# Banks shared between Winograd products, later operand conversions and an earlier last sum in the down-projection of a one-core trunk kernel

## The chip, the cores and the metric

One core of a Trainium2 chip runs the whole program. The metric is the device time of one execution in microseconds (us). The engines are named as in the profile: PE (matrix multiplies, with PEld for its weight loads), DVE (vector), ACT (scalar), POOL (GpSimd) and SP (DMA issue).

## The reference, cut to what matters

One layer over 1024 tokens with 1024 channels: attention and a gated merge, then a gated MLP with a short convolution, then a final RMSNorm. The change lies in the last two steps:

```python
D_MODEL, SEQ, D_FF, EPS = 1024, 1024, 2816, 1e-6
# u: gate and value after the up-projection and the causal convolution
x = x + (jax.nn.silu(gate) * val) @ w_down[l]     # (1024, 2816) @ (2816, 1024)
...
def rmsnorm(x, w):
    y = x * lax.rsqrt(jnp.mean(x * x, axis=-1, keepdims=True) + EPS)
    return y * w
return rmsnorm(x, norm_final_w)
```

## The kernel before, in words

Everything is kept transposed: channels on the 128 partitions, tokens along the free dimension, and the 1024 tokens are two halves of 512. The float32 operands are each split into a high and a low part: ACT casts the high part (lines 127, 157, 175 for weights, 831 for hidden activations) and DVE subtracts it to get the low part (lines 128, 158, 177 and 832). Such a cast and subtraction together are called a **conversion** below. One product of four 128-row blocks then takes 12 matmuls of 128x512: high by high, high by low and low by high for each block (`product`, lines 918 to 920; with `low_last` the low weights come last, lines 912 and 914).

The down-projection (`down`) sums over 22 blocks of 128 hidden rows. Six blocks are done plainly (line 1157), then two **groups** of eight blocks are done by Winograd's form of Strassen's scheme. In it an output **pair** m (0 to 3) holds the channel blocks m and m+4, and the four quarters of its result are `col(m, 0)`, `col(m, 1)`, `col(m + 4, 0)` and `col(m + 4, 1)` of the accumulator `x3` (tile `x`, 128x512 each). Seven products replace eight: P1 = A11·B11, P2 = A12·B21, P3 = S4·B22, P4 = A22·T4, P5 = S1·T1, P6 = S2·T2, P7 = S3·T3. The A and S are weights and weight differences (POOL makes the S, lines 103 to 109 and 148 to 151), the B and T are hidden activations and their differences.

Every product lands in a PSUM bank. There are four banks of tag `d` and four of tag `y`. An **addition** is one DVE instruction that adds a bank into a quarter of `x3`. In the first group the loop before has done P1 and P2 with two additions a pair; the loop over pairs in the diff does P5, P6, P3, P4, P7. P1, P6 and P7 of a pair pile up in its `y` bank and are read out on the way; P5, P3 and P4 each have a `d` bank of their own. That loop has seven additions a pair: two at line 1235, one each at 1237, 1240 and 1243, and two at 1248.

Between these, `diffs(k)` forms the differences of the second group's activations (lines 1203 to 1206), and `prepare` queues the second group's conversions. Their 28 buffers are the ones that the first group's operands hold, so each conversion waits until PE has read a given operand for the last time: B11 takes T1's place, B21 T2's, T4 B22's, T2 T4's, T3 T3's own; T1 and B22 of the second group take the raw buffers. The weight buffers `wh` (A11/A12 and A22) and `sh` (S) have two copies each, the raw weight buffers three, the POOL sums `c` two. So a weight's conversion waits for PE, a DMA for conversions, and POOL for DMA and DVE.

The order of each engine's instructions is set by the framework's scheduler from the order in the code, with priorities and `issue_after` edges; each engine then runs its queue strictly in that order. At the end, `last_norm` sums squares over channels with matmuls against a column of ones (line 218), makes the reciprocal root on DVE and POOL (lines 225 and 227), spreads it by transposes (line 233) and multiplies the result (line 1361). The first half of the tokens is normalized beside the second group's last products, the second half in two quarters of 256 tokens. ACT takes the squares (line 1261) and the weighting by the norm's vector (line 1265).

Of the kernel before, what the change touches and what calls it, by code (L numbers as in the profile page):

```python
# [10 lines left out]
F32 = mybir.dt.float32  # L11
# [33 lines left out]
class Trunk:  # L45
# [92 lines left out]
    def second_pair(self, src, m):  # L138

        nc = self.nc  # L140
        raws = []
        for x in src:
            raws.append(self.tl(self.wp, [P, 8, P], "raw", bufs=RAW))
            nc.sync.dma_start(raws[-1], x)
        g, v = (r.rearrange("p (k a) c -> p a k c", a=2) for r in raws)
        sa, sb = (self.tl(self.sfp[0], [P, 2, 4, P], self.sfp[1]) for _ in range(2))
        tt = nc.gpsimd.tensor_tensor
        tt(sa[:, 0], v[:, 0], v[:, 1], ALU.add)
        tt(sb[:, 0], sa[:, 0], g[:, 0], ALU.subtract)
        tt(sb[:, 1], g[:, 0], v[:, 0], ALU.subtract)  # L150
        tt(sa[:, 1], g[:, 1], sb[:, 0], ALU.subtract)
        nc.sync.dma_start(self.sd[m], sa.rearrange("p a k c -> p (a k) c"))
        ops = {}
        for pool, h, l, x, names in ((self.wp, "wh", "wl", g, ("A11", "A12")), (self.uw, "sh", "sl", sb, ("S2", "S3")), (self.wp, "wh", "wl", v[:, 1:2], ("A22",))):
            hi = self.tl(pool, [P, len(names), 4, P], h, F32R)
            lo = self.tl(pool, [P, len(names), 4, P], l, F32R)
            nc.scalar.copy(hi, x)
            nc.vector.tensor_tensor(lo, x, hi.bitcast(F32), ALU.subtract)
            for i, name in enumerate(names):
                ops[name] = hi[:, i], lo[:, i]  # L160
        return ops
# [59 lines left out]
    def rstd_cols(self, ssq_ps, n, width):  # L221

        nc = self.nc
        ms = self.tl(self.st, [P, 8], "ms")
        nc.vector.tensor_scalar(ms[:, :n], ssq_ps[:, :n], 1.0 / width, EPS, ALU.mult, ALU.add)  # L225
        rs = self.tl(self.st, [P, 8], "rs")
        self.pow = nc.gpsimd.tensor_tensor(rs[:, :n], ms[:, :n], self.mhalf[:, :n], ALU.pow)  # L227
        return rs
# [821 lines left out]
    def sums_h(self, k):  # L1050

        b11, b12, b22, b21 = (self.raw_h(N1 + j, hf) for j, hf in ((k, 0), (k, 1), (k + 4, 1), (k + 4, 0)))
        tt = self.nc.vector.tensor_tensor
        tt(b11, b12, b11, ALU.subtract)
        self.B["T1", k] = self.parts_h(b11)
        tt(b12, b22, b12, ALU.subtract)
        tt(b22, b22, b11, ALU.subtract)
        self.B["T2", k] = self.parts_h(b22)
        self.B["T3", k] = self.parts_h(b12)
        tt(b21, b22, b21, ALU.subtract)  # L1060
        self.B["T4", k] = self.parts_h(b21)

    def glu(self, j, w, us, tp, after):
# [44 lines left out]
    def down(self):  # L1108

        nc, tc = self.nc, self.tc  # L1110
        with ExitStack() as ctx:
# [80 lines left out]
            def load(k):  # L1192

                r = self.slot(base + 2 * k), self.slot(base + 2 * k + 1)
                for o in range(2):
                    nc.sync.dma_start(r[o].rearrange("p a b -> p (a b)"), self.hd[N2 + 2 * k + o])
                raws[k] = [x[:, i] for x in r for i in range(2)]

            def diffs(k, after):

                b11, b12, b21, b22 = raws[k]
                with tc.issue_after(after.ins):
                    tt(b11, b12, b11, ALU.subtract)
                    tt(b12, b22, b12, ALU.subtract)
                    tt(b22, b22, b11, ALU.subtract)
                    tt(b21, b22, b21, ALU.subtract)
# [20 lines left out]

            for k in range(4):
                load(k)
            for m, y in enumerate(ys):  # L1230
                w = self.next_w()
                ps = bank(0)
                self.product(ps, w["S1"], "T1")
                for x in (col(m, 1), col(m + 4, 1)):
                    tt(x, x, ps, ALU.add)
                self.product(y, w["S2"], "T2", first=False, skip=True)
                tt(col(m, 1), col(m, 1), y, ALU.add)
                ps = bank(0)
                self.product(ps, w["S4"], "B22")
                tt(col(m, 1), col(m, 1), ps, ALU.add)  # L1240
                ps = bank(0)
                self.product(ps, w["A22"], "T4")
                i = tt(col(m + 4, 0), col(m + 4, 0), ps, ALU.subtract)
                if m in (1, 2):
                    diffs(2 * m - 1, i)
                self.product(y, w["S3"], "T3", first=False, skip=True)
                for hf in range(2):
                    i = tt(col(m + 4, hf), col(m + 4, hf), y, ALU.add)
                if m < 2:
                    diffs(2 * m, i)  # L1250
            prepare(24)
            q = H2 // 2
            seen = []
# [1 line left out]
            def evac(ps, m, hf, a=0, b=H2, last=False):  # L1255

                x = x3[:, m, hf * H2 + a:hf * H2 + b]
                tt(x, x, ps, ALU.add)
                sum_ = box[hf][:, a:b]
                sq = box[2 + len(seen) % 2][:, a:b] if hf in seen else sum_  # L1260
                nc.scalar.activation(sq, x, AF.Square)
# [3 lines left out]
                nc.scalar.mul(x, x, self.vecs[:, C_NO + m:C_NO + m + 1])  # L1265
                return sq

            ys, ws = [], []

# [5 lines left out]
            for m in range(4):  # L1275
                w = self.next_w()
                ws.append(w)
                y, ps = bank(1), bank(0)
                ys.append(y)
                self.product(y, w["A11"], "2B11", skip=True, low_last=True)  # L1280
                tt(col(m, 0), col(m, 0), y, ALU.add)
# [12 lines left out]
            tail = self.last_norm(psD, [box[0]], x3, 0, 0, H2, ((0, 2, nc.vector), (6, 8, nc.gpsimd), (2, 4, nc.vector), (4, 6, nc.vector)))  # L1294
# [134 lines left out]
```

## Time and profile before

| | |
|---|---|
| time, median of 3 runs | 1343.62 us (1343.31 to 1343.88) |
| time of the profiled execution | 1343.35 us |
| its span in the profile | 1341.1 us, so 2.25 us lie around it |
| PE busy | 1321.7 us (99% of the span) |
| DVE, ACT, POOL busy | 1065.8, 621.7, 495.6 us |
| mean granted PE clock | 0.995 |

PE is nearly always busy; it is idle for longer than a matmul only at the start, in the passage from the first to the second group (1250 to 1259 us) and at the end (from 1330 us). In rows of the timeline the first two numbers are the start and the duration in us; a bracket holds the idle time before the row and what ended it.

### The profile page before, as it was taken

How to read it: one execution, taken by the hardware profiler on the slowest of the kernel's cores; microseconds unless marked ns; L12 is line 12 of the kernel's file. 1: busy time of each engine (PE TensorE's matmuls, PEld its weight loads, DVE VectorE, ACT ScalarE, POOL GpSimd, SP SyncE). 2: the span in 40 equal slices, each digit the busy share in tenths (PEclk: the TensorE clock that was granted, in tenths of full speed). 3: DMA queues.
4: the chain of work that ended last, by engine and by line, in shares of the span. 5: the costliest groups of instructions: out<-in, count | busy, mean ns of one | idle time of the engine just before them, and what ended most of it. 6: DMA issues, size and time to landing. Idle time of an engine off the chain costs nothing.

```text
span 1341.1 us, 17306 instructions
## 1 busy us (share of the span) xinstructions
PE 1321.7 (99%) x6264; PEld 1097.4 (82%) x6264; DVE 1065.8 (79%) x1603; ACT 621.7 (46%) x1019; POOL 495.6 (37%) x365
## 2 busy tenths in 40 slices
PE   7999999999999999999999999999999999999997
PEld 6888888888888778878888888888888888888787
DVE  8847775289889876465678999999999987869975
ACT  8432232276667665333454444334444434323443
POOL 0336552000102124641446555655556510224412
PEclk9999999999999999999999999999999999999998
DMA  6423443966553235334423222222222239562333
GB/s 258 148 104 150 149 157 141 254 174 188 143 138 130 93 121 200 138 110 157 141 96 108 65 93 90 83 81 77 95 79 90 75 116 330 202 246 71 113 115 126
DMA packets 63045, 182.64 MB, mean 136 GB/s; under 512 B 6896, under 2 KB 15216, under 8 KB 62960
## 3 DMA queue, kind: packets, MB, share of 16 engines
q1 hardware_dynamic: 51504, 164.13, 37.3%
q10 hardware_dynamic: 11456, 17.41, 3.6%
q8 instruction: 49, 0.80, 0.2%
q14 instruction: 36, 0.29, 0.1%
HBM read 130.66 MB, written 50.86 MB: 135 GB/s over the span
## 4 chain that ended last, share of the span: by engine, by line
PE 86%; DVE 5%; POOL 4%; DMA 2%; issue 2%; ACT 1%; POOLq 0%; SPq 0%; ACTq 0%; DVEq 0%
PE t L920 13%; PE t L919 13%; PE t L918 13%; PE g L210 3%; PE g L211 3%; PE g L212 3%; PE t L912 3%; PE sc L634 3%; PE y L1157 2%; PE d L1157 2%; PE sc L212 2%; PE sc L210 2%; PE sc L211 2%; DMA gr<-gd 2%; PE d L918 2%
## 5 line engine op out<-in xcount | busy, mean ns | idle before, releaser
L1087 ACT ACTIVATE c<-us,vecs 128x512 f32<-128x512 f32 x80 | 61.3, 781 | 132.3 <-POOL us L1081 128.3
L1089 DVE SCALAR_TENSOR_TENSOR c<-us,vecs,c 128x512 f32<-128x512 f32 x160 | 110.4, 747 | 8.6 <-ACT c L1087 8.5
L1081 POOL TENSOR_TENSOR us<-us,rstd 128x1024 f32<-128x1024 f32 x38 | 99.6, 2642 | 4.5 <-DVE us L467 2.4
L128 DVE TENSOR_TENSOR sl<-sf,sh 128x1024 fp32r<-128x1024 f32 x62 | 87.6, 1416 | 11.5 <-ACT sh L127 11.5
L127 ACT CAST sh<-sf 128x1024 fp32r<-128x1024 f32 x62 | 63.4, 1048 | 60.4 <-PE t L919 44.0
L177 DVE TENSOR_TENSOR wl<-raw,wh 128x1024 fp32r<-128x1024 f32 (+2 forms) x46 | 57.7, 1255 | 30.2 <-ACT wh L175 18.9
L128 DVE TENSOR_TENSOR wl<-raw,wh 128x1024 fp32r<-128x1024 f32 (+1 forms) x35 | 75.9, 2169 | 3.7 <-ACT wh L127 3.6
L103 POOL TENSOR_TENSOR sf<-rv 128x512 f32<-128x512 f32 x30 | 41.3, 1377 | 100.9 <-DVE sl L128 57.8
L175 ACT CAST wh<-raw 128x1024 fp32r<-128x1024 f32 (+2 forms) x46 | 46.0, 1001 | 62.6 <-PE sc L211 30.5
L210 PE MATMUL g<-xh,wh 128*128 128x512 f32 x176 | 70.7, 402 | 0.1
L212 PE MATMUL g<-xh,wl 128*128 128x512 f32 x176 | 70.4, 400 | 0.0
L211 PE MATMUL g<-xl,wh 128*128 128x512 f32 x176 | 70.3, 400 | 0.0
L108 POOL TENSOR_TENSOR sf<-raw,rv 128x512 f32<-128x512 f32 x30 | 40.7, 1356 | 65.4 <-DVE sl L128 65.4
L617 POOL MEMSET aT<- 128x128 f32 x32 | 6.1, 205 | 151.5 <-PE t L663 63.2
L638 DVE CUSTOM_DVE_ANT_0 L<-sc,bias 128x128 f32<-128x128 f32 (+7 forms) x64 | 47.7, 751 | 17.0 <-PE sc L634 13.7
L639 ACT ACTIVATE L<-L,sm 128x128 f32<-128x128 f32 (+7 forms) x64 | 49.6, 778 | 20.0 <-DVE sm L638 13.5
L792 POOL TENSOR_TENSOR gr<-gr,rstd 128x1024 f32<-128x1024 f32 x16 | 40.4, 2533 | 41.2 <-DMA gr<-gd 40.9
L1091 ACT ACTIVATE c<-c 128x512 f32<-128x512 f32 x40 | 24.0, 600 | 60.7 <-DVE c L1089 60.7
L128 DVE TENSOR_TENSOR wl<-rv,wh 128x512 fp32r<-128x512 f32 x30 | 49.2, 1640 | 3.5 <-ACT wh L127 3.5
L634 PE MATMUL sc<-u,u 128*128 128x512 f32 (+2 forms) x192 | 49.7, 358 | 0.0
L212 PE MATMUL sc<-mh,wl 128*128 128x512 f32 x126 | 49.1, 390 | 0.3 <-DVE wl L177 0.3
L227 POOL TENSOR_TENSOR rs<-ms,mhalf 128x8 f32<-128x8 f32 (+2 forms) x9 | 13.6, 1517 | 96.5 <-DVE ms L225 85.9
(522 smaller groups left out, 4429.6 us busy)
## 6 DMA issues: line engine op xcount, KB each, us to landing
u<-qd SPq DMA_DIRECT2D x72, 256.0 KB, 6.0
raw<-in_w_in SPq DMA_DIRECT2D x25, 512.0 KB, 4.1
raw<-in_w_up SPq DMA_DIRECT2D x23, 512.0 KB, 3.5
hr<-hd SPq DMA_DIRECT2D x46, 256.0 KB, 5.2
hd<-c SPq DMA_DIRECT2D x22, 512.0 KB, 2.6
rv<-in_w_up SPq DMA_DIRECT2D x21, 512.0 KB, 3.5
raw<-in_w_down SPq DMA_DIRECT2D x19, 512.0 KB, 4.1
gr<-gd SPq DMA_DIRECT2D x16, 512.0 KB, 3.5
```

The source lines that it names most:

```text
L127: i = nc.scalar.copy(hi, src)
L128: j = nc.vector.tensor_tensor(lo, src, hi.bitcast(F32), ALU.subtract)
L210: nc.tensor.matmul(ps, wh[:, kc + o, :], ah, start=first and n == 0, stop=False)
L211: nc.tensor.matmul(ps, wh[:, kc + o, :], al, start=False, stop=False)
L212: nc.tensor.matmul(ps, wl[:, kc + o, :], ah, start=False, stop=last and n == len(kcs) - 1)
L634: nc.tensor.matmul(sc[:, lo + n0:lo + n1], qs, k[c][part][:, n0:n1], start=part == 0, stop=part == 1)
L918: nc.tensor.matmul(ps, ah[:, k, :], bh, start=first and n == 0, stop=False, skip_group_check=skip)
L919: nc.tensor.matmul(ps, ah[:, k, :], bl, start=False, stop=False, skip_group_check=skip)
L920: i = nc.tensor.matmul(ps, al[:, k, :], bh, start=False, stop=last and n == len(ks) - 1, skip_group_check=skip)
L1081: (nc.vector if j == 0 else nc.gpsimd).tensor_tensor(u[:, 2:], u[:, 2:], self.rstd, ALU.mult)
L1087: nc.scalar.activation(c, u[:, o + 2:o + 2 + H2], AF.Identity, bias=self.vecs[:, C_CB + m:C_CB + m + 1], scale=col(m, 2))
L1089: nc.vector.scalar_tensor_tensor(c, u[:, o + k:o + k + H2], col(m, k), c, ALU.mult, ALU.add)
```

## The change: what it does

- **First group.** P5 is added to one quarter only, and P3 then accumulates onto P5's bank, whose sum is added to `col(m, 1)`. P4 accumulates onto P7's bank `y`, one pair later (`fourth(m - 1)`); its sum is the only addition to `col(m + 4, 0)`. T4 gets the opposite sign, so that it is added. With the two additions of the loop before this makes seven a pair; pair 3 has P4 in a bank of its own and one more. The loop goes from 28 additions to 21. PE's order of products becomes P5, P6, P4 of the pair before, P3, P7.
- **diffs** are placed at other points of that loop.
- **Second group.** `prepare(4)` queues T1's and B22's conversions behind those of the weights of the last pair asked for (`self.made`).
- **The end.** In the last two quarters, the weighting of the last two blocks is queued behind the last square. The ones-matmuls go over the squares first and over the two 128-token columns second, with one bank for each column, and the mean is taken by two small DVE instructions.

The core of the diff:

```diff
@@ second_pair
-            nc.scalar.copy(hi, x)
-            nc.vector.tensor_tensor(lo, x, hi.bitcast(F32), ALU.subtract)
+            self.made = nc.scalar.copy(hi, x), nc.vector.tensor_tensor(lo, x, hi.bitcast(F32), ALU.subtract)
@@ rstd_cols
-        nc.vector.tensor_scalar(ms[:, :n], ssq_ps[:, :n], 1.0 / width, EPS, ALU.mult, ALU.add)
+        parts = ssq_ps if isinstance(ssq_ps, list) else [ssq_ps[:, :n]]
+        w = n // len(parts)
+        for i, x in enumerate(parts):
+            nc.vector.tensor_scalar(ms[:, i * w:(i + 1) * w], x, 1.0 / width, EPS, ALU.mult, ALU.add)
@@ sums_h
-        tt(b21, b22, b21, ALU.subtract)
+        tt(b21, b21, b22, ALU.subtract)
@@ down, first group
+            def put(ps, *at):
+                for m, hf in at:
+                    i = tt(col(m, hf), col(m, hf), ps, ALU.add)
+                return i
+
+            def fourth(m):
+                ps = ys[m] if m < 3 else bank(0)
+                self.product(ps, ws[m]["A22"], "T4", first=m == 3, skip=m < 3)
+                put(ps, (m + 4, 0))
+
             for m, y in enumerate(ys):
                 w = self.next_w()
+                ws.append(w)
                 ps = bank(0)
-                self.product(ps, w["S1"], "T1")
-                for x in (col(m, 1), col(m + 4, 1)):
-                    tt(x, x, ps, ALU.add)
+                self.product(ps, w["S1"], "T1", skip=True)
+                put(ps, (m + 4, 1))
                 self.product(y, w["S2"], "T2", first=False, skip=True)
-                tt(col(m, 1), col(m, 1), y, ALU.add)
-                ps = bank(0)
-                self.product(ps, w["S4"], "B22")
-                tt(col(m, 1), col(m, 1), ps, ALU.add)
-                ps = bank(0)
-                self.product(ps, w["A22"], "T4")
-                i = tt(col(m + 4, 0), col(m + 4, 0), ps, ALU.subtract)
+                i = put(y, (m, 1))
+                if m == 0:
+                    diffs(0, i)
+                else:
+                    fourth(m - 1)
+                if m == 3:
+                    fourth(m)
+                self.product(ps, w["S4"], "B22", first=False, skip=True)
+                i = put(ps, (m, 1))
                 if m in (1, 2):
-                    diffs(2 * m - 1, i)
+                    diffs(m + 1, i)
                 self.product(y, w["S3"], "T3", first=False, skip=True)
-                for hf in range(2):
-                    i = tt(col(m + 4, hf), col(m + 4, hf), y, ALU.add)
-                if m < 2:
-                    diffs(2 * m, i)
+                i = put(y, (m + 4, 1), *([(m + 4, 0)] if m == 3 else []))
+                if m == 0:
+                    diffs(1, i)
@@ down, second group
-                prepare(4)
+                with ExitStack() as queue:
+                    for i in self.made:
+                        queue.enter_context(tc.issue_after(i.ins))
+                    prepare(4)
@@ down, last two quarters (evac now returns the weighting for later where last is set)
-                sqs = [box[1][:, a:b], third(2, ws[2], p[0], a, b, True)]
+                ends = [third(2, ws[2], p[0], a, b, True)]
                 if not a:
                     step()
-                sqs.append(third(3, ws[3], p[1], a, b, True))
+                ends.append(third(3, ws[3], p[1], a, b, True))
+                with tc.issue_after(self.square.ins):
+                    for _, weigh in ends:
+                        weigh()
+                sqs = [box[1][:, a:b]] + [x for x, _ in ends]
@@ last_norm
-            ssq = self.tl(psD, [P, H2], "d")
-            self.col_sums(ssq, sqs, n, 0)
+            ...
+            ssq = [self.tl(psD, [P, H2], t)[:, 0:1] for t in "dy"]
+            for k, sq in enumerate(sqs):
+                for i, x in enumerate(ssq):
+                    nc.tensor.matmul(x, sq[:, i * P:(i + 1) * P], self.ones, start=k == 0, stop=k == len(sqs) - 1)
```

The instructions move with it. On DVE, at the end of the second group's first conversions, the order before is this (`h` are activations, with T3's last two first; `wl` and `sl` are low parts of the next pair's weights; `x<-x,y` at line 1281 is the addition of P1 of pair 0, which PE's P6 on the same bank waits for):

```order
L832 TENSOR_TENSOR h_1896_10966<-h_1814_10503,h_1896_10966 128x512
L832 TENSOR_TENSOR h_1897_10969<-h_1816_10507,h_1897_10969 128x512
L158 TENSOR_TENSOR wl_10988<-raw_10976,wh_10987 128x1024
L158 TENSOR_TENSOR sl_10992<-c_10981,sh_10991 128x1024
L158 TENSOR_TENSOR wl_10996<-raw_10978,wh_10995 128x512
L1281 TENSOR_TENSOR x_9784<-x_9784,y_10999 128x512
L1288 TENSOR_TENSOR x_9784<-x_9784,d_11029 128x512
```

The same place of the changed kernel, where the addition is at line 1298:

```order
L834 TENSOR_TENSOR h_1889_10952<-h_1814_10503,h_1889_10952 128x512
L834 TENSOR_TENSOR h_1890_10955<-h_1816_10507,h_1890_10955 128x512
L157 TENSOR_TENSOR sl_10978<-c_10967,sh_10977 128x1024
L157 TENSOR_TENSOR wl_10974<-raw_10962,wh_10973 128x1024
L1298 TENSOR_TENSOR x_9784<-x_9784,y_10985 128x512
L1305 TENSOR_TENSOR x_9784<-x_9784,d_11015 128x512
L157 TENSOR_TENSOR wl_10982<-raw_10964,wh_10981 128x512
```

P1's addition stands one weight subtraction earlier, and still behind all the conversions of T4, T2 and T3.

On PE, where P6 of pair 0 begins in the second group, the order before is this (`d_11092` is P2 of pair 1, `y_10999` the bank of pair 0):

```order
L920 MATMUL d_11092<-h_1879_10918,wl_10988 128x512
L918 MATMUL d_11092<-h_1881_10923,wh_10987 128x512
L919 MATMUL d_11092<-h_1881_10923,wh_10987 128x512
L920 MATMUL d_11092<-h_1881_10923,wl_10988 128x512
L918 MATMUL d_11092<-h_1883_10928,wh_10987 128x512
L918 MATMUL y_10999<-h_1890_10948,sh_10818 128x512
```

In the changed kernel P6's bank is `y_10985`, and P1 of pair 1 is `y_11077`:

```order
L922 MATMUL d_11015<-h_1882_10931,wl_10798 128x512
L914 MATMUL y_11077<-h_1864_10884,wh_10973 128x512 x2
L914 MATMUL y_11077<-h_1866_10889,wh_10973 128x512
L920 MATMUL y_10985<-h_1883_10934,sh_10793 128x512
L921 MATMUL y_10985<-h_1883_10934,sh_10793 128x512
```

Before, P6 of pair 0 came behind all 12 matmuls of pair 1's P1 and 7 of its P2; now it comes behind 3 of P1, so it is asked for 16 matmuls earlier.

On ACT, the casts of pair 1's weights (`wh`) and of T1 (the four `h` that read the raw buffers 1810, 1812, 1814 and 1816) stood mixed:

```order
L831 CAST h_1897_10969<-h_1816_10507 128x512
L831 CAST h_1915_11056<-h_1810_10495 128x512
L831 CAST h_1916_11059<-h_1812_10499 128x512
L157 CAST wh_10987<-raw_10976 128x1024
L831 CAST h_1917_11062<-h_1814_10503 128x512
L831 CAST h_1918_11065<-h_1816_10507 128x512
L157 CAST wh_10995<-raw_10978 128x512
```

Now the weights stand ahead of all four:

```order
L833 CAST h_1890_10955<-h_1816_10507 128x512
L157 CAST wh_10973<-raw_10962 128x1024
L157 CAST wh_10981<-raw_10964 128x512
L833 CAST h_1908_11042<-h_1810_10495 128x512
L833 CAST h_1909_11045<-h_1812_10499 128x512
L833 CAST h_1910_11048<-h_1814_10503 128x512
L833 CAST h_1911_11051<-h_1816_10507 128x512
```

Both weight casts of pair 1 moved ahead of T1's four.

More of the change, by code (lines that the diff above doesn't have):

```diff
@@ L1229, in down @@
                 load(k)
+            ws = []
+            def put(ps, *at):
[6 more added lines that the diff above has]
+                put(ps, (m + 4, 0))
             for m, y in enumerate(ys):
                 w = self.next_w()
+                ws.append(w)
                 ps = bank(0)
-                self.product(ps, w["S1"], "T1")
-                for x in (col(m, 1), col(m + 4, 1)):
-                    tt(x, x, ps, ALU.add)
+                self.product(ps, w["S1"], "T1", skip=True)
+                put(ps, (m + 4, 1))
                 self.product(y, w["S2"], "T2", first=False, skip=True)
-                tt(col(m, 1), col(m, 1), y, ALU.add)
-                ps = bank(0)
-                self.product(ps, w["S4"], "B22")
-                tt(col(m, 1), col(m, 1), ps, ALU.add)
-                ps = bank(0)
-                self.product(ps, w["A22"], "T4")
-                i = tt(col(m + 4, 0), col(m + 4, 0), ps, ALU.subtract)
+                i = put(y, (m, 1))
[7 more added lines that the diff above has]
+                i = put(ps, (m, 1))
                 if m in (1, 2):
-                    diffs(2 * m - 1, i)
+                    diffs(m + 1, i)
                 self.product(y, w["S3"], "T3", first=False, skip=True)
-                for hf in range(2):
-                    i = tt(col(m + 4, hf), col(m + 4, hf), y, ALU.add)
-                if m < 2:
-                    diffs(2 * m, i)
+                i = put(y, (m + 4, 1), *([(m + 4, 0)] if m == 3 else []))
+                if m == 0:
+                    diffs(1, i)
             prepare(24)
@@ L1260, in evac @@
                 sq = box[2 + len(seen) % 2][:, a:b] if hf in seen else sum_
-                nc.scalar.activation(sq, x, AF.Square)
+                self.square = nc.scalar.activation(sq, x, AF.Square)
                 if hf in seen and not last:
@@ L1264, in evac @@
                 seen.append(hf)
-                nc.scalar.mul(x, x, self.vecs[:, C_NO + m:C_NO + m + 1])
-                return sq
+                weigh = lambda: nc.scalar.mul(x, x, self.vecs[:, C_NO + m:C_NO + m + 1])
+                if last:
+                    return sq, weigh
+                weigh()
             ys, ws = [], []
@@ L1323, in down @@
                     step()
-                sqs = [box[1][:, a:b], third(2, ws[2], p[0], a, b, True)]
+                ends = [third(2, ws[2], p[0], a, b, True)]
                 if not a:
                     step()
-                sqs.append(third(3, ws[3], p[1], a, b, True))
+                ends.append(third(3, ws[3], p[1], a, b, True))
+                with tc.issue_after(self.square.ins):
+                    for _, weigh in ends:
+                        weigh()
+                sqs = [box[1][:, a:b]] + [x for x, _ in ends]
                 assert not tail
@@ L1341, in sums @@
         def sums():
-            ssq = self.tl(psD, [P, H2], "d")
-            self.col_sums(ssq, sqs, n, 0)
+            if n == NB // 2:
+                ssq = self.tl(psD, [P, H2], "d")
+                self.col_sums(ssq, sqs, n, 0)
+                box.append(self.rstd_cols([ssq[:, :n]], n, D))
+                return
+            ssq = [self.tl(psD, [P, H2], t)[:, 0:1] for t in "dy"]
+            for k, sq in enumerate(sqs):
+                for i, x in enumerate(ssq):
+                    nc.tensor.matmul(x, sq[:, i * P:(i + 1) * P], self.ones, start=k == 0, stop=k == len(sqs) - 1)
             box.append(self.rstd_cols(ssq, n, D))
```

## The prediction

> **What bounds the kernel now.** I read the page's head first, then PE's waits from 1130 us on (the down-projection and the end), then the timelines of PE, DVE, ACT and POOL around the longest of these waits.
>
> ```profile
> span 1341.1 us, 17306 instructions
> PE 1321.7 (99%) x6264; PEld 1097.4 (82%) x6264; DVE 1065.8 (79%) x1603; ACT 621.7 (46%) x1019; POOL 495.6 (37%) x365
> PE y L912 <- ACT wh L157: 1.9, 1, 1.9
> PE d L233 <- POOL rs L227: 1.0, 1, 1.0
> PE d L218 <- ACT hr L1261: 0.8, 2, 0.5
> ```
>
> PE is the bound, so only time that PE loses can be saved. The change adds and removes no matmul, so I look for what PE lost in the part that it touches. A product of 12 matmuls takes 2.72 us, read from the starts of the first two products of the first group. The rows after these are PE's around the longest wait, and then one window of 20 us and four of 1 us; a window lists the busy time of PE, PEld, DVE, ACT and POOL, and its last number but two is the granted clock.
>
> ```profile
> 1190.08 0.39 PE L918 MATMUL d<-h,sh 128*128 128x512 f32 x1
> 1192.80 0.39 PE L918 MATMUL y<-h,sh 128*128 128x512 f32 x1
> 1253.45 0.39 PE L920 MATMUL d<-h,wl 128*128 128x512 f32 x1
> 1255.70 2.52 PE L912 MATMUL y<-h,wh 128*128 128x512 f32 x8 [1.86 <-ACT wh L157]
> ...
> 1262.06 0.39 PE L918 MATMUL y<-h,sh 128*128 128x512 f32 x1
> 1240.00:1260.00 20.00, 17.68 (x71) 13.41 (x70) 20.00 (x28) 10.48 (x18) 6.33 (x4) 0.93 0.32 106
> 1257.00:1258.00 1.00, 1.00 (x4) 0.79 (x3) 1.00 (x3) 0.21 (x1) 0.00 (x0) 0.62 0.00 0
> 1258.00:1259.00 1.00, 0.85 (x3) 0.20 (x2) 1.00 (x2) 0.00 (x0) 0.00 (x0) 0.50 0.00 0
> 1259.00:1260.00 1.00, 1.00 (x3) 0.81 (x4) 1.00 (x2) 0.00 (x0) 0.00 (x0) 0.50 0.26 37
> 1260.00:1261.00 1.00, 1.00 (x5) 0.76 (x4) 1.00 (x3) 0.00 (x0) 0.00 (x0) 0.67 0.73 221
> ```
>
> The row at 1262.06 is the first matmul of the second group's P6 of pair 0. Ahead of it, from 1190.08 on, stand 20 products of the first group and 55 matmuls of the second, 295 in all. Without a stall they take 295 x 2.72 / 12 = 66.9 us, to 1256.95. PE came at 1262.06, so it had lost **5.1 us**. Part of this is the wait, part a slow clock after it: in the four windows the clock lacks 0.38 + 0.50 + 0.50 + 0.33 = 1.7 us.
>
> Why was PE late? It waited for the cast of pair 1's weights, which stood on ACT behind two casts of T1, which waited for DVE. DVE's rows there, and the POOL rows that slowed it:
>
> ```profile
> 1208.52 1.77 DVE L1204 TENSOR_TENSOR h<-h,h 128x512 f32<-128x512 f32 x1
> 1208.02 1.74 POOL L109 TENSOR_TENSOR c<-raw,c 128x512 f32<-128x512 f32 x1
> 1231.32 1.05 ACT L127 CAST sh<-c 128x1024 fp32r<-128x1024 f32 x1 [2.08 <-PE y L919]
> 1232.63 1.22 DVE L128 TENSOR_TENSOR sl<-c,sh 128x1024 fp32r<-128x1024 f32 x1
> 1234.97 1.19 DVE L1206 TENSOR_TENSOR h<-h 128x512 f32<-128x512 f32 x1
> 1238.47 1.72 DVE L158 TENSOR_TENSOR sl<-c,sh 128x1024 fp32r<-128x1024 f32 x1
> 1250.30 7.30 DVE L832 TENSOR_TENSOR h<-h,h 128x512 fp32r<-128x512 f32 x12
> 1257.53 1.21 DVE L158 TENSOR_TENSOR wl<-raw,wh 128x1024 fp32r<-128x1024 f32 x1
> 1258.66 1.21 DVE L158 TENSOR_TENSOR sl<-c,sh 128x1024 fp32r<-128x1024 f32 x1
> 1260.40 0.68 DVE L1281 TENSOR_TENSOR x<-x,y 128x512 f32<-128x512 f32 x1
> 1253.48 1.22 ACT L831 CAST h<-h 128x512 fp32r<-128x512 f32 x2 [3.23 <-DVE h L832]
> 1254.61 1.04 ACT L157 CAST wh<-raw 128x1024 fp32r<-128x1024 f32 x1
> ```
>
> In the window from 1240 to 1260 DVE is busy for all of the 20 us. Undisturbed, a 512-wide row takes 0.60 us (7.30 / 12) and a 1024-wide one 1.13 (1258.66 - 1257.53). While POOL runs, a DVE row that reads SBUF alone takes up to 1.77: it waits for POOL's instruction to end (1208.02 + 1.74 = 1209.76) and then runs its 0.5. So in this passage PE follows DVE's queue, and DVE's queue follows POOL.
>
> **The first group.** The loop's additions:
>
> ```profile
> L1248 DVE TENSOR_TENSOR x<-x,y 128x512 f32<-128x512 f32 x8 | 5.3, 680 | 2.0 <-PE y L920 2.0
> L1235 DVE TENSOR_TENSOR x<-x,d 128x512 f32<-128x512 f32 x8 | 5.3, 676 | 0.6 <-PE d L920 0.6
> L1240 DVE TENSOR_TENSOR x<-x,d 128x512 f32<-128x512 f32 x4 | 2.7, 684 | 0.8 <-PE d L920 0.6
> L1243 DVE TENSOR_TENSOR x<-x,d 128x512 f32<-128x512 f32 x4 | 2.7, 682 | 2.0 <-PE d L920 2.0
> L1237 DVE TENSOR_TENSOR x<-x,y 128x512 f32<-128x512 f32 x4 | 2.7, 677 | 1.4 <-PE y L920 1.4
> ```
>
> 28 become 21, so DVE is spared 7 x 0.60 = 4.2 us. The new accumulations make PE wait for additions: P3 for P5's, P4 for P7's. Two products (5.44 us) lie between in pairs 1 to 3 and one (2.72 us) in pair 0, where DVE's queue is still short; an addition is 0.68. I take this wait at nothing. If DVE were late it would be some tenths at each place, and a late DVE would show more in the passage.
>
> **The passage.** Now DVE's queue of the changed kernel, row by row at these prices, up to P1's addition, which P6 of pair 0 waits for. It starts with the low part of pair 3's S3/S4. Its cast waits for pair 2's P7, the 14th product: 1190.08 + 14 x 2.72 = 1228.2. Before, that low part ended 2.53 us after such a cast began (1232.63 + 1.22 - 1231.32), so it ends at **1230.7**. Behind it stand 20 low parts of activations, 8 additions and one low part of 512, and 4 low parts of 1024: 29 x 0.60 + 4 x 1.13 = 21.9 us.
>
> POOL's price is the unknown one. Before, from the end of the same kind of row (1233.85) to the end of P1's addition (1261.08) 27.2 us passed. In them stood 33 rows of 512 and 3 of 1024, so 23.2 us of work, and the same seven POOL instructions (three of pair 0, four of pair 1): they cost 4.0 us. The bounds: both POOL sequences cost what the first did, 0.6 + 0.5 by the rows at 1234.97 and 1238.47, so 2.2; or each of the seven holds up a row for 1.17 (1.77 - 0.60), so 8.2. I take 4.0, since it is the same seven in front of the same conversions.
>
> So P1's addition ends at 1230.7 + 21.9 + 4.0 = **1256.6**. PE asks for it after 20 + 3 products and 3 matmuls, at 1190.08 + 62.6 + 0.7 = **1253.3**. It stalls **3.3 us**. The cast of pair 1's weights, now ahead of T1's, stops being what comes last, and P1's addition is late next. The 4.2 us that DVE is spared are nearly used up by PE asking 16 matmuls (3.6 us) earlier. Behind this stall PE is likely to run at half clock again, as it did after an idle of 2.25 us (1253.45 to 1255.70): 1.7 us as measured, nothing to 3.4 as bounds.
>
> The row first: an idle of 2.25 us was enough to halve the clock for 3.4 us, from 1257.2 to 1260.7. [...]
>
> The middle: 3.3 + 1.7 - 5.1 = **-0.1 us**. T1's and B22's conversions behind the weights cost nothing: PE reads them only after the loop over the second group's pairs.
>
> **The end.** Here the chain is last addition, squares, ones-matmuls, mean, root:
>
> ```profile
> 1330.06 0.78 DVE L1258 TENSOR_TENSOR x<-x,d 128x256 f32<-128x256 f32 x2
> 1330.51 0.42 ACT L1261 ACTIVATE hr<-x 128x256 f32<-128x256 f32 x1 [1.72 <-DVE x L1258]
> 1330.95 0.51 ACT L1265 ACTIVATE x<-x,vecs 128x256 f32<-128x256 f32 x1
> 1331.37 0.40 ACT L1261 ACTIVATE hr<-x 128x256 f32<-128x256 f32 x1
> 1330.97 0.38 PE L218 MATMUL d<-ones,hr 128*128 128x1 f32 x2 [0.33 <-ACT hr L1261]
> 1331.82 1.43 PE L218 MATMUL d<-ones,hr 128*128 128x1 f32 x8 [0.46 <-ACT hr L1261]
> 1333.29 0.16 DVE L225 TENSOR_SCALAR ms<-d 128x2 f32<-128x2 f32 x1 [2.45 <-PE d L218]
> ```
>
> The second square no longer waits for the weighting: it starts at the addition's end, 1330.9, and ends at 1331.3 instead of 1331.8. Each ones-matmul instruction takes 0.18 us (1.43 / 8). The four for the first square run from 1330.97 to 1331.7, the four for the second to 1332.4, where before the last ended at 1333.25: 0.85 us sooner. The second mean instruction gives back under 0.1. So **-0.8 us**, between -0.5 (if PE's clock is lower) and -1.1 (if the matmuls wait for the square alone).
>
> **The sum.** -0.1 - 0.8 = -0.9 us against the profiled execution's 1343.35: **1342.5 us**. That execution lies 0.27 below the median of the runs shown. 0.2%, 2.7 us, is about what a measurement of this kernel can tell from no change; so the forecast is no change by that bound. Stall and clock together decide: faster by 2.7 needs at most 5.1 + 0.8 - 2.7 = 3.2 us, slower by 2.7 at least 8.6.
>
> **The rivals.**
> 1. *POOL costs DVE little, and the clock holds.* With 2.2 us P1's addition ends at 1254.8, PE stalls 1.5 us, less than the 2.25 that halved the clock, and the clock costs nothing: 1.5 - 5.1 - 0.8 = -4.4, **1338.9**. For it: the first POOL sequence cost 1.1, since additions, which read PSUM, ran beside it. Against it: with fewer additions, more of the rows beside POOL are low parts that it can hold up. Chance 0.36, because a stall just under 2.25 also drops the clock's 1.7 at one stroke.
> 2. *DVE meets POOL at each instruction* (slower). Three of the seven POOL instructions now fall right after 1230.7, where DVE has four low parts in its queue, and the other four come when pair 1's raw weights have landed, among the low parts of T4 and T2. At 8.2 us the addition ends at 1260.8, PE stalls 7.5 us, and with 1.7 of slow clock the sum is 7.5 + 1.7 - 5.1 - 0.8 = +3.3, **1346.7**. It decides from a POOL price of about 7.6 us on. Chance 0.22.
> 3. The forecast, between them: chance 0.42. Its own range, for POOL prices of 3.0 to 5.5 us and a clock price of 0.9 to 2.4, is 1340.7 to 1344.7.
>
> **The numbers.** Faster 0.36, within 0.2% 0.42, slower 0.22, from these three. The range reaches to both rivals, 1338.9 to 1346.7.
>
> **What would show it.** In the changed profile: 21 additions in the loop; no PE wait there for them; the second group's first P6 starting right behind an addition `x<-x,y` near 1256.6, after a gap of about 3 us in P1 of pair 1; a granted clock near 0.5 for some 3 us behind it; the last ones-matmul 0.8 us after the one for the first square. I am wrong if PE waits for a weight cast there, if the gap is under 2 us, or if PE has stopped in the first group for an addition.

## The result and the profile after

The changed kernel takes 1346.03 us (median of 21 runs, 1344.71 to 1348.57), the kernel before 1343.67 (21 runs, 1341.56 to 1347.05). The ratio is 1.0015, with a 95% interval of 1.0009 to 1.0021: 1.2 to 2.8 us slower. The forecast was 0.9 us faster. The profiled execution took 1346.61 us, its span 1344.4.

PE's waits from 1130 us on, in the changed kernel:

```profile
PE y L920 <- DVE x L1298: 4.9, 1, 4.9
PE d L235 <- POOL rs L229: 1.0, 1, 1.0
PE d L1374 <- ACT hr L1276: 0.2, 1, 0.2
```

The wait for a weight cast (`wh L157`) is gone. In its place stands one wait of 4.9 us for line 1298, P1's addition. PE's first S1 matmul (the first matmul of the first group, from which times are counted below), its rows around the wait, and four windows with the granted clock (last number but two):

```profile
1192.26 0.39 PE L920 MATMUL d<-h,sh 128*128 128x512 f32 x1
1254.82 0.84 PE L914 MATMUL y<-h,wh 128*128 128x512 f32 x3
1260.55 0.80 PE L920 MATMUL y<-h,sh 128*128 128x512 f32 x1 [4.89 <-DVE x L1298]
1264.99 0.58 PE L921 MATMUL y<-h,sh 128*128 128x512 f32 x1
1258.00:1259.00 1.00, 0.00 (x0) 0.00 (x0) 1.00 (x2) 0.00 (x0) 0.00 (x0) 0.78 0.00 0
1261.00:1262.00 1.00, 1.00 (x3) 0.71 (x3) 1.00 (x3) 0.00 (x0) 0.00 (x0) 0.50 0.60 135
1264.00:1265.00 1.00, 1.00 (x4) 0.71 (x4) 0.00 (x0) 0.00 (x0) 1.00 (x1) 0.50 0.85 324
1265.00:1266.00 1.00, 1.00 (x5) 0.82 (x4) 0.16 (x1) 0.00 (x0) 1.00 (x2) 0.81 0.28 111
```

P6 should have followed 3 x 0.227 us (2.72 / 12 each) behind 1254.82, at 1255.50. It came at 1260.55, **5.05 us** late. Then nearly all of its 12 matmuls, up to 1265.4, ran at half clock: 4.85 us for the first eleven where 2.50 is normal, so **2.4 us** lost. The kernel before lost 5.1 us in this passage, this one 7.4 (5.05 + 2.4).

DVE's and POOL's rows ahead of that addition:

```profile
1231.75 1.22 DVE L128 TENSOR_TENSOR sl<-c,sh 128x1024 fp32r<-128x1024 f32 x1
1234.08 4.59 DVE L834 TENSOR_TENSOR h<-hr,h 128x512 fp32r<-128x512 f32 x3
1247.47 4.75 DVE L834 TENSOR_TENSOR h<-h,h 128x512 fp32r<-128x512 f32 x3
1253.34 4.29 DVE L834 TENSOR_TENSOR h<-h,h 128x512 fp32r<-128x512 f32 x7
1259.82 0.68 DVE L1298 TENSOR_TENSOR x<-x,y 128x512 f32<-128x512 f32 x1
1233.10 1.62 POOL L149 TENSOR_TENSOR c<-c,raw 128x512 f32<-128x512 f32 x1 [4.75 <-issue]
1236.38 1.74 POOL L151 TENSOR_TENSOR c<-raw,c 128x512 f32<-128x512 f32 x1
1246.99 1.28 POOL L148 TENSOR_TENSOR c<-raw 128x512 f32<-128x512 f32 x1 [8.87 <-DMA raw<-in_w_down]
1251.75 1.63 POOL L151 TENSOR_TENSOR c<-raw,c 128x512 f32<-128x512 f32 x1
```

Seven low parts take 4.29 us where POOL is idle. Three take 4.59 and 4.75 where it works. DVE never rests from 1231.75 to 1260.5.

At the end of the program, first the kernel before and then the changed one (first ones-matmul of the last quarter, and the last root on POOL):

```profile
1330.29 0.35 PE L218 MATMUL d<-ones,hr 128*128 128x1 f32 x2
1333.53 0.70 POOL L227 TENSOR_TENSOR rs<-ms,mhalf 128x2 f32<-128x2 f32 x1 [3.67 <-DVE ms L225]
```

```profile
1334.71 0.36 PE L1374 MATMUL d<-ones,hr 128*128 128x1 f32 x2
1336.16 0.36 PE L1374 MATMUL y<-ones,hr 128*128 128x1 f32 x2
1336.80 0.70 POOL L229 TENSOR_TENSOR rs<-ms,mhalf 128x2 f32<-128x2 f32 x1 [2.44 <-DVE ms L227]
```

2.09 us instead of 3.24: the end gained **1.15 us**.

### The profile page after: what moved, and what is told of

The parts are those of the page before. It is cut to its first block, busy times and chain, and to the rows that moved or that the text cites. A ratio compares the mean times of both kernels' runs of the same rounds, so it can differ in the third digit from the quotient of the medians.

```text
span 1344.4 us, 17299 instructions
## 1 busy us (share of the span) xinstructions
PE 1322.4 (98%) x6264; PEld 1098.2 (82%) x6264; DVE 1065.8 (79%) x1598; ACT 621.9 (46%) x1019; POOL 493.1 (37%) x365
## 4 chain that ended last, share of the span: by engine, by line
PE 84%; DVE 5%; POOL 4%; DMA 4%; issue 1%; ACT 1%; POOLq 0%; SPq 0%; ACTq 0%; DVEq 0%
PE t L921 13%; PE t L922 13%; PE t L920 13%; PE t L914 3%; PE g L209 3%; PE sc L636 3%; PE g L210 3%; PE g L211 3%; PE sc L211 2%; PE sc L210 2%; PE sc L209 2%; DMA gr<-gd 2%; PE d L1159 2%; PE y L1159 2%; PE d L920 2%; PE d L922 2%
## 5 line engine op out<-in xcount | busy, mean ns | idle before, releaser
L108 POOL TENSOR_TENSOR sf<-raw,rv 128x512 f32<-128x512 f32 x30 | 40.7, 1357 | 65.4 <-DVE sl L128 65.4
```

## The experiments

A single profile starts its first group at a different moment each time. Where the code ahead of it and the first group are the old ones, the first S1 matmul starts at 1190.08, 1192.24, 1191.67, 1193.30 and 1190.18 us. With the changed first group it starts at 1192.26, 1192.16, 1189.16, 1191.06, 1192.04, 1191.73, 1193.52 and 1190.85. The means are 1191.5 and 1191.6, so the 2.2 us by which the changed kernel's profile is behind there are scatter. I therefore read each profile from its first S1 matmul to its last root on POOL, and call this the **stretch**: 143.45 us before, 144.54 after.

| kernel | ratio to before (95%) | stretch | wait ahead of P6 of pair 0 |
|---|---|---|---|
| changed | 1.0015 (1.0009-1.0021) | 144.54 | 4.9, half clock |
| e1 end alone | 0.9991 (0.9982-0.9999) | 142.04 | as before |
| e2 first group alone | 1.0026 (1.0017-1.0035) | 145.57 | 2.0 + 2.7, half clock |
| e3 changed, old end | 1.0021 (1.0012-1.0030) | 146.02 | 5.0, half clock |
| e4 P1's addition early | 1.0017 (1.0008-1.0025) | 145.42 | 1.1; 3.6 later, half clock |
| e5 same, B22 late | 0.9971 (0.9960-0.9982) | 138.51 | 1.0 |
| e6 B22 late alone | 1.0010 (0.9999-1.0021) | 144.19 | 4.9, half clock |
| e7 e5 with old first group | 0.9974 (0.9964-0.9984) | 139.21 | none; 0.7 for a weight |
| e8 changed, part of POOL's work left out | 0.9953 (0.9936-0.9970) | 137.08 | none |
| e9 PE kept busy | 1.0009 (1.0000-1.0018) | 142.96 | 1.0 |
| e10 e7, addition later | 0.9993 (0.9982-1.0003) | 140.44 | 2.0 |
| e11 before, part of POOL's work left out | 0.9968 (0.9955-0.9982) | 139.00 | none |

**The parts of the change.** e1 is the kernel before with the end alone. Its core, with the weightings behind the last square:

```diff
-            ssq = self.tl(psD, [P, H2], "d")
-            self.col_sums(ssq, sqs, n, 0)
+            ssq = [self.tl(psD, [P, H2], t)[:, 0:1] for t in "dy"]
+            for k, sq in enumerate(sqs):
+                for i, x in enumerate(ssq):
+                    nc.tensor.matmul(x, sq[:, i * P:(i + 1) * P], self.ones, start=k == 0, stop=k == len(sqs) - 1)
```

> The kernel before with the change's end alone (squares first, ones-matmuls over the squares with a bank for each column). Theory A (the end is worth what its rows say: the chain from the last addition to the root is shorter by the weighting and by four ones-matmuls): 0.8 to 1.2 us less than the kernel before; from the first ones-matmul of the last quarter to the root 2.1 us instead of 3.2. Rival B (what the end gains comes back in the multiplications and stores behind it): within 0.3 us of the kernel before, with the stretch behind the root longer by as much.

Measured: 1342.55 us against 1343.77, 1.2 less (0.1 to 2.4 by the interval); the stretch is 1.4 shorter, from the last root to the end of the span it is 7.6 us in both, and PE still waits 1.8 us for the weight cast in the passage. Theory A holds.

e2 has the first group's hunk alone, e3 that and the queue edit, with the old end:

```diff
+                with ExitStack() as queue:
+                    for i in self.made:
+                        queue.enter_context(tc.issue_after(i.ins))
+                    prepare(4)
```

> The kernel before with the change's first group alone (shared banks, 21 additions, diffs moved); T1's and B22's conversions stay ahead of the next weights, the end is old. Theory A (the loss is that P6 of the second group's pair 0 waits for P1's addition, which stands in DVE's queue behind conversions that POOL holds up; the casts of pair 1's weights have slack): the same as the next kernel within 0.5 us, so some 2.4 us more than the kernel before; a stall of about 5 us ahead of P6 with an addition as its releaser. Rival B (the edit on the weight casts is what matters there): PE waits for a cast of pair 1's weights as before, and the time differs from the next kernel by over 1 us. Rival C (the shared banks cost PE in the first group): PE waits for additions inside the first group, over 0.5 us in all.

> The changed kernel with the old end. Theory A: the changed kernel's time plus the end's 1.1 us, 2.3 to 3.5 us more than the kernel before; stall 5 us and 12 matmuls at half clock (2.4 us lost) where the kernel before lost 5.1. Rival B (the loss arises ahead of the first group, where the profile of the changed kernel ran 2.2 us later than that of the kernel before): the first S1 matmul stands near 1192 again, and the stretch from there to the end of the span is within 0.5 us of the kernel before's 151.0.

Measured: 1347.19 and 1347.25 us, 3.4 and 3.5 more than the kernel before. PE's waits of e2:

```profile
PE y L918 <- DVE x L1294: 2.7, 1, 2.7
PE y L912 <- ACT wh L157: 2.0, 1, 2.0
```

Without the queue edit the 5 us come in two pieces, first for the cast and then for the addition; with it, in one. The time is the same as that of e3, as A has it, and the addition comes last in any case. But B's wait is there: the casts did not have the slack that A gave them, and the 2.4 us that A forecast for e2 lie only just inside its interval (2.3 to 4.7). C is out: PE waits for no addition inside the first group in any of these profiles. B of e3 is out too: its first group starts at 1189.16, the earliest of all, and the loss behind it is the same.

**P1's addition moved forward.** e4:

```diff
-                tt(col(m, 0), col(m, 0), y, ALU.add)
+                with tc.high_priority(200 if m == 0 else 0):
+                    tt(col(m, 0), col(m, 0), y, ALU.add)
```

> The changed kernel with one addition moved in DVE's queue: P1's of the second group's pair 0 stands right behind T2's last low part, ahead of T3's four low parts and two low parts of weights; PE then has P6 of pair 0 directly behind P4. Theory A: the addition ends 4.7 us sooner (4 x 0.60 + 2 x 1.13), near 1255.9 in the times of the changed kernel's profile; PE asks at 1254.8, so it stalls 1.1 us, keeps its clock, and then waits some tenths for pair 1's low weights: 5 to 6 us less than the changed kernel, 3 to 4 less than the kernel before. Rival B (the stall only moves: PE next waits for pair 1's low weights or T3 for as long, or its clock drops all the same): within 1.5 us of the changed kernel. Rival C (the loss is not in the passage): the same as the changed kernel.

Measured: 1345.90 us, no gain: B as to the time. But the first stall went as A had it, and another one came. PE, DVE and ACT in e4:

```profile
1254.88 0.50 PE L920 MATMUL y<-h,sh 128*128 128x512 f32 x1 [1.10 <-DVE x L1299]
1280.73 0.80 PE L920 MATMUL y<-h,sh 128*128 128x512 f32 x1 [3.63 <-DVE x L1308]
1277.72 2.36 DVE L834 TENSOR_TENSOR h<-hr,h 128x512 fp32r<-128x512 f32 x2 [4.08 <-ACT h L833]
1280.00 0.68 DVE L1308 TENSOR_TENSOR x<-x,y 128x512 f32<-128x512 f32 x1
1277.07 2.57 ACT L833 CAST h<-hr 128x512 fp32r<-128x512 f32 x4 [5.03 <-DMA hr<-hd]
```

P7 of pair 1 waits for the addition of P6 of pair 1 (line 1308). That stands in DVE's queue behind two low parts of B22, which wait for the cast and the DMA. In the changed kernel this chain is there too, and PE is simply too late to meet it: the same addition ends at 1282.41, and PE comes to P7 of pair 1 at 1284.04. e5 takes it away, e6 makes that edit alone:

```diff
-                    prepare(4)
+                    if m in (0, 2):
+                        prepare(4)
```

> The kernel with P1's addition moved forward, and B22's four conversions of the second group queued one pair later (behind pair 3's weights, where they stood behind pair 2's). In the kernel with the addition moved alone, PE's stall ahead of P6 of pair 0 fell from 4.9 us to 1.1 at a full clock, but PE then waited 3.6 us for the addition of P6 of pair 1, which stood in DVE's queue behind two of these conversions, and they for the DMA of B22. Theory A (that second wait is all that swallowed the gain): it goes, with the half clock behind it; 5 to 6 us less than that kernel, so near 1340, 3 to 4 us less than the kernel before. Rival B (the DMAs of B22 and of the last pair's weights limit PE there wherever the conversions stand): a third wait of over 2 us in the second group, and a time within 1.5 us of the changed kernel.

> The changed kernel with B22's conversions one pair later and nothing else. Theory A: PE is not waiting for them in the changed kernel, since the stall ahead of P6 has made PE late enough: within 0.5 us of the changed kernel in the stretch from the first S1 matmul to the end of the span (152.1 us), still with the 5 us stall. Rival B (the place of these conversions is itself what costs): 2 us or more less than the changed kernel.

Measured: e5 1339.85 us against 1344.17 of the kernel before, **2.4 to 5.4 us less** by the interval: it beats both kernels. Its only new wait in PE:

```profile
PE y L920 <- DVE x L1299: 1.0, 1, 1.0
```

e6: 1344.59, with the same 4.9 us stall. By the yardstick of the expectation, from the first S1 matmul to the end of the span, it takes 151.4 us against 152.1: 0.8 less, so A's 0.5 is missed, and B's 2 is far off. 0.4 of the 0.8 lies ahead of the last root (stretch 144.19), and the intervals of the two times overlap. So the B22 edit alone is worth little, under 1 us in these profiles; it pays once the stall ahead of it is gone.

**What the first group's 7 additions are worth.** e7 is e5 with the first group of before:

> The kernel with both moves (P1's addition forward, B22's conversions later), but with the first group of the kernel before: 28 additions, no shared banks. Theory A (the 7 additions spared are worth their 4.2 us of DVE, and are seen once PE asks for an addition that stands right behind T2's low parts): P1's addition ends later, and PE stalls 2 to 4 us ahead of P6 of pair 0 instead of 1.1, perhaps with some half clock: 2 to 5 us more than with the changed first group. Rival B (the first group's change is worth nothing, because DVE catches up in any case): the same within 1 us.

Measured: 1340.07, and a stretch 0.7 us longer, as B has it. A's stall did not come, but the comparison was not clean: the same priority put P1's addition behind T4's third low part there, five low parts further forward than in e5. e10 holds it behind T2's last one, as in e5:

```diff
-                with tc.high_priority(200 if m == 0 else 0):
+                with tc.high_priority(200 if m == 0 else 0), tc.issue_after(self.t2.ins):
```

> The kernel with the first group of before and both moves, but with P1's addition behind T2's last low part, where it stands in the kernel with the changed first group; without that it stood five low parts further ahead. Theory A (7 additions spared are 4.2 us of DVE, but the addition's place in the queue can make up for that): P1's addition ends 3.0 us later, PE stalls 2.5 to 3 us ahead of P6 of pair 0 and runs at half clock behind it; 4 to 5 us more from the first S1 matmul to the last root than the 139.2 of the kernel with the addition further ahead. Rival B (the first group's change is worth nothing even so): within 1 us of that kernel.

Measured: 1342.25 us, stretch 140.44. P1's addition in e5, in e7 and in e10, PE's row of e10, and its window that holds the stall and P6:

```profile
1255.03 0.68 DVE L1299 TENSOR_TENSOR x<-x,y 128x512 f32<-128x512 f32 x1
1253.46 0.68 DVE L1286 TENSOR_TENSOR x<-x,y 128x512 f32<-128x512 f32 x1
1258.37 0.67 DVE L1288 TENSOR_TENSOR x<-x,y 128x512 f32<-128x512 f32 x1
1259.10 0.50 PE L920 MATMUL y<-h,sh 128*128 128x512 f32 x1 [2.03 <-DVE x L1288]
1256.00:1264.00 8.00, 5.97 (x27) 4.62 (x26) 8.00 (x13) 2.70 (x5) 0.00 (x0) 1.00 0.25 73
```

Counted from the first S1 matmul, the addition ends at 63.7 us in e5, 62.5 in e7 and 65.7 in e10. So in e10 it ends 3.3 us later than in e7, and PE stalls 2.0 us, less than my 2.5 to 3, at full clock. The stretch is 1.2 us longer than that of e7: neither A's 4 to 5 nor B's 1. At the same place in the queue the changed first group brings the addition 2.1 us forward (e5 against e10), half of the 4.2 us of work that it spares, and saves 1.9 us of the stretch (140.44 - 138.51); five low parts of place make up for 1.2 of them. These are single profiles; the ratios of e10 and e5 lie 3.0 us apart, and their intervals touch.

**POOL's price.** e8 leaves POOL's eight sums of pairs 0 and 1 out of the changed kernel, e11 out of the kernel before:

```diff
+        if m < 2:
+            sa, sb = g, v
+        else:
             ...
-        nc.sync.dma_start(self.sd[m], sa.rearrange("p a k c -> p (a k) c"))
+        nc.sync.dma_start(self.sd[m], raws[0] if m < 2 else sa.rearrange("p a k c -> p (a k) c"))
```

> The changed kernel without POOL's weight differences of the second group's pairs 0 and 1: their place is taken by the raw weights, so those eight POOL instructions are left out and the differences are not computed. Theory A (POOL holds up DVE's low parts by 5.6 us in the passage): P1's addition ends that much sooner, at the time when PE asks for it; the stall ahead of P6 of pair 0 is under 1 us at a full clock, and three low parts of activations take 1.9 us where they took 4.6. A wait further on, as for B22's DMA, may take part of the 7 us back. Rival B (DVE's rows are long there for another reason, and POOL's timing is a coincidence): the rows stay long, and the stall stays over 3 us.

> The kernel before without POOL's weight differences of the second group's pairs 0 and 1 (left out, raw weights in their place). The forecast read a POOL price of 4.0 us out of the kernel before and took the same for the changed kernel, where leaving POOL out moved P1's addition by 5.3 us. Theory A (the price depends on what DVE does beside POOL's instructions: rows that read PSUM run through, rows that read SBUF alone wait): here the addition moves by about 4 us, from 71.0 us after the first S1 matmul to about 67, and the wait for the weight cast goes; 4.5 to 5.5 us less than the kernel before. Rival B (POOL's price is the same in both kernels, and the 4.0 was misread): the addition moves by 5.3 us or more.

Measured: e8 1336.53 us, e11 1339.46. DVE's rows of e8 in the places of those of 4.59 and 4.75 us, then P1's addition there and in e11:

```profile
1235.35 1.89 DVE L837 TENSOR_TENSOR h<-hr,h 128x512 fp32r<-128x512 f32 x3
1246.19 1.89 DVE L837 TENSOR_TENSOR h<-h,h 128x512 fp32r<-128x512 f32 x3
1255.81 0.68 DVE L1301 TENSOR_TENSOR x<-x,y 128x512 f32<-128x512 f32 x1
```

```profile
1256.52 0.68 DVE L1284 TENSOR_TENSOR x<-x,y 128x512 f32<-128x512 f32 x1
```

In e8 (first S1 matmul at 1193.52) the addition ends 62.97 us after it, in the changed kernel 68.24: POOL costs **5.3 us**. In e11 (1190.18) it ends at 67.02, in the kernel before at 71.00: **4.0 us**. A holds in both as to the price: the three low parts shrink to 1.89 us, and the price is not one price. In time e11 is 4.3 us below the kernel before by the ratio, just under A's 4.5.

In the changed kernel's rows the DVE and POOL instructions end in turn. The second of its three low parts from 1247.47 on, and the POOL instructions beside it:

```profile
1248.75 1.77 DVE L834 TENSOR_TENSOR h<-h,h 128x512 fp32r<-128x512 f32 x1
1248.23 1.74 POOL L150 TENSOR_TENSOR c<-raw,raw 128x512 f32<-128x512 f32 x1
1249.94 1.73 POOL L149 TENSOR_TENSOR c<-c,raw 128x512 f32<-128x512 f32 x1
```

POOL's first instruction ends at 1249.97, the low part 0.55 us later; the next POOL instruction then ends 1.15 us behind the low part, and the third low part (to 1252.22) again 0.55 us behind that. What ties their ends together is not shown. An addition, which reads PSUM, takes its usual 0.68 us beside POOL (the one at 1233.48, while POOL works from 1233.10 to 1234.72).

**The clock's price.** e9 gives PE work ahead of the place where it stalls:

```diff
+                for _ in range(0 if m else 20):
+                    nc.tensor.matmul(ps, w["A22"][0][:, 0, :], self.B["2T4", 0][0], start=True, stop=True, skip_group_check=True)
                 self.product(ps, w["A22"], "2T4")
```

> The changed kernel with 20 matmuls added: the first matmul of P4 of the second group's pair 0 is issued 20 times more ahead of that product, on its own bank and overwritten by it, so that PE works for 20 x 0.227 = 4.5 us where it stalls. The scheduler then puts P1's first three matmuls of pair 1 behind P6 instead of ahead of it. Theory A (the stall is set by DVE's queue, and the half clock behind it, 2.4 us, is the price of the idle time): P6 of pair 0 starts as long after the first S1 matmul as before (68.3 us), behind a stall of some 1.2 us, and runs at full clock; 2.4 - 0.7 = 1.7 us less from the first S1 matmul to the last root than the changed kernel's 144.5, so about 1344.3, although PE does more. Rival B (the low clock there has another cause than idling, such as load or the kind of matmul): P6's 12 matmuls again take 0.43 us each, and the time is 0.7 us above the changed kernel's.

PE's rows of e9, the added matmuls first, and the window around them:

```profile
1250.69 4.70 PE L1305 MATMUL d<-h,wh 128*128 128x512 f32 x20
1259.15 0.50 PE L920 MATMUL y<-h,sh 128*128 128x512 f32 x1 [1.04 <-DVE x L1298]
1259.48 0.39 PE L921 MATMUL y<-h,sh 128*128 128x512 f32 x1
1250.00:1270.00 20.00, 18.96 (x84) 15.36 (x83) 18.50 (x24) 7.94 (x12) 8.78 (x6) 1.00 0.15 54
```

Measured: 1344.93 us, stretch 142.96, 1.6 us shorter than the changed kernel's with 20 matmuls more. P6 starts 68.30 us after the first S1 matmul (1190.85), the same as without them (68.29). A holds by the trace: the end of the stall is set by DVE, and with 1.04 us of idle time ahead of P6 instead of 4.89 P6 runs at 1.00 instead of 0.50. In the times it is not shown: the intervals of e9 and of the changed kernel overlap.

## Why the prediction was wrong

- **What bounds the passage, and what is late next**: right. P1's addition took the place of the weight cast, P6 starts right behind it and runs at half clock (0.50), and there are 21 additions in the loop with no wait of PE for them.
- **DVE's queue, start and work**: right. The low part of pair 3's S3/S4 ends 40.7 us after the first S1 matmul (forecast 40.6). From there to P1's addition e8, without POOL, takes 22.3 us (forecast 21.9).
- **POOL's price**: the step that failed. "I take 4.0, since it is the same seven in front of the same conversions." The 4.0 was read rightly (e11), but did not carry over: it is 5.3 (e8) to 5.6 (27.5 - 21.9) in the changed kernel, at the upper end of the 3.0 to 5.5 that the forecast allowed itself. The instructions are the same, what DVE does beside them is not. At the second POOL sequence both lose 2.9 us (4.0 - 1.1 before; 4.75 - 1.89 after). At the first one two rows lost 0.6 and 0.5 in the kernel before, among additions; in the changed one three low parts stand there in a row and lose 2.7 (4.59 - 1.89). The forecast named this against rival 1, and still kept 4.0. P1's addition ended 68.2 us after the first S1 matmul instead of 66.5, and the stall became 5.05 us instead of 3.3.
- **The clock**: right that it halves, but it cost 2.4 us instead of 1.7, the upper end of its own range. The windows of the changed kernel (0.78 and 0.81 at the two ends) put the half clock at 1258.56 to 1265.38, 6.8 us where the forecast carried over the 3.4 of the kernel before; the first 2.0 of them fell into the stall and cost nothing. In the kernel before PE still ran about 1.5 us at full clock behind its wait. The "idle of 2.25 us" that the forecast compared stalls with runs from the start of a matmul; the idle time in the row is 1.86.
- **The end**: -1.15 instead of -0.8, just beyond the bound (-1.1) that had the ones-matmuls wait for the square alone.
- **T1's and B22's conversions "cost nothing"**: for B22's true of the changed kernel to under 1 us (e6), but not for the reason given. DVE runs B22's low parts ahead of an addition that PE needs; they cost so little only because the stall had made PE late. In e4 they cost a wait of 3.6 us.
- **The sum**: 5.05 + 2.4 - 5.1 - 1.15 = +1.2 us in the two profiles, against -0.9 forecast. Of the 2.1 between them the stall makes +1.75 (1.3 to 1.6 of it POOL's price), the clock +0.7 and the end -0.35. POOL's price alone turns the sign, the clock alone does not. The measured difference is 2.0 (1.2 to 2.8). What of the remaining 0.8 is real stays open. Over the twelve kernels of the table the measured difference to the kernel before lies 0.8 us on average above that of the stretches, so the one profile of before may be on the slow side there; that was not shown.
- **The rivals**: rival 2 had the mechanism and the sign (DVE meets POOL more often, PE stalls longer), with too high a price, 8.2, and so a stall of 7.5 us. That its 1346.7 nearly equals the measured times is luck: in the two profiles its mechanism came to +1.2 us, not +3.3, and the profiled execution's 1346.61 holds the 2.2 us of a later start. Rival 1 is out.
- **"The 4.2 us that DVE is spared are nearly used up"**: right, and the way out was in the order rows shown ahead of the prediction: P1's addition behind four low parts of T3 and two of weights that PE does not need before P6. Moved ahead of them, and with B22's conversions later, the kernel beats both.

## What to carry to other kernels

A stall that one engine's queue sets is priced by what stands in that queue at that moment: a price read from another order of the same instructions need not carry over, as here, where POOL and DVE held each other up and 4.0 us became 5.3. Look at what stands between the needed instruction and the front of the queue before sparing work elsewhere: moving one addition past work that nobody waited for yet, with the next wait taken away too, was worth 6.0 us of the stretch (144.54 - 138.51), sparing seven additions 1.9. When a move gains nothing, read the next wait before dropping it; here it hid a second one, and both had to go.

## What the runs showed of the hardware

The length of an idle time did not decide alone whether PE's clock halved. In e1 it halved behind a wait of 1.84 us; in e10 it did not behind one of 2.03 (its window above has clock 1.00). The row of e1, and the windows in which its half clock begins and ends:

```profile
1257.72 2.57 PE L915 MATMUL y<-h,wh 128*128 128x512 f32 x8 [1.84 <-ACT wh L157]
1259.00:1260.00 1.00, 1.00 (x4) 0.84 (x3) 1.00 (x3) 0.23 (x1) 0.00 (x0) 0.59 0.00 0
1262.00:1263.00 1.00, 1.00 (x5) 0.79 (x4) 1.00 (x2) 0.00 (x0) 0.00 (x0) 0.70 0.61 172
```

What decides it besides is not shown.

In the four kernels whose windows show both ends of a half clock, it lasted 3.4 or 6.8 us. In e1 the windows give 1259.18 to 1262.60, 3.4 us, as in the kernel before; in the changed kernel, with 4.9 us of idle time, 1258.56 to 1265.38, 6.8 us, and as long in e4 behind its 3.6 us (1280.1 to 1286.9). Why one or the other is not shown.

POOL's instructions get longer too. Two like ones of the changed kernel, the first beside a DVE row that reads SBUF alone (line 1206), the second beside an addition and then an idle DVE:

```profile
1206.78 0.68 DVE L1206 TENSOR_TENSOR h<-h,h 128x512 f32<-128x512 f32 x1
1206.93 1.67 POOL L108 TENSOR_TENSOR c<-raw,raw 128x512 f32<-128x512 f32 x1 [1.17 <-DVE sl L128]
1220.85 1.28 POOL L108 TENSOR_TENSOR c<-raw,raw 128x512 f32<-128x512 f32 x1 [1.77 <-DVE sl L128]
```

POOL takes 1.67 us against 1.28; the DVE row had begun 0.15 us before the first one.
